# Late weight forms and retention operands given out in parts behind a bank's copy, and halo loads put into the chain of loads

## The chip, the core and the metric

The kernel runs on one core of a Trainium2 chip. The metric is the device time of one execution in microseconds (us); lower is better. Engines are named as in the profile: PE is TensorE (matmuls; PEld its weight loads), ACT is ScalarE, DVE is VectorE, SP the engine that issues most DMAs.

## What is computed

One block over 16 meta tokens and 512 tokens of width 1024: a recurrent branch, a retention branch with four heads, two gates that mix them, an out-projection and a gated feed-forward part with a short convolution. Cut to what matters here:

```python
xn = rms_norm(h, norm_mix_g[l])
z = xn @ w_in[l]
u_rnn, u_gate, q, k, v, g_ret, ga, gb = jnp.split(z, IN_SPLITS, axis=-1)
...
o = retention(q, k, v.reshape(bsz, t, RET_HEADS, RET_DV))
o_b = head_rms(o).reshape(bsz, t, RET_HEADS * RET_DV) * jax.nn.silu(g_ret)
mixed = (jax.nn.sigmoid(ga) * (o_a @ w_branch_rnn[l])
         + jax.nn.sigmoid(gb) * (o_b @ w_branch_ret[l]))
h = h + mixed @ w_out[l]
xn = rms_norm(h, norm_ffn_g[l])
up = causal_dwconv(xn @ w_up[l], ffn_conv_w[l], ffn_conv_b[l])
gate, val = jnp.split(up, 2, axis=-1)
h = h + (jax.nn.gelu(gate) * val) @ w_down[l]
```

## The kernel before

Every f32 operand is held as two f16 halves, hi and lo, and a product is three matmuls (hi by hi, hi by lo, lo by hi). `split` (L90) makes a pair of halves: ACT writes hi (L91), then DVE writes lo (L92). It is used for the weights, for activations and for the values `v`.

**Weights.** They come in units of up to 1 MB. `load` (L96) issues each unit's DMA on SP into a `raw` tile and keeps these loads in one chain of order; a load can go out once its `raw` tile is free. Each unit has a list of steps, and `tick` hands out the next step if not too many tiles (`ahead`) would be held; `get(u)` hands out all that unit u still needs.

**Fast units.** The gates (g_ret, ga, gb), the branch product with w_branch_ret and the down-projection multiply 2x2 blocks with seven products in place of eight. The weights of such a unit need five steps (`fast_steps`, L212): the split of B11, the split of B21 and B22, three sums on DVE in `raw` (L231 to L233), and then two *late forms*: T1 with T3, and T4 with T2, each a split of 128x1024. `fast_products` (L768) is the generator of the seven products P1, P7, P6, P2, P5, P3, P4. P1, P6, P5 and P3 all add into one PSUM bank, `pa`; after P1 and P6 `keep` copies it on ACT to `kept`, after P5 to `last` (L781), and the next of these products may only write the bank when that copy is through. A product of a gate is 12 matmuls of 257 columns; `mix_products` (L970), the product with w_branch_ret, takes two units and has 24 matmuls in each.

**Gates of the retention.** `gated(h)` (L916) runs two gate units of head h and puts the four groups of `retention_out(h+1)` (24 matmuls `ps<-sc,v` each) between their products. At a unit's end `finish` multiplies the gate into the retention's output (L887), and after the second of the two calls `ob_forms` (L893) makes the operands of the later product: four subtractions on DVE (L897 to L900) and four splits into `ob` tiles. `values(h)` (L816) makes `v` in five blocks, each split out of a PSUM bank. Head 3's gates stand among the mixing gates: `gate_a` and `gate_b` call gate products, a branch product and, in `gate_b`, `mix_products`.

**Order.** Each engine runs its own instructions in order. The order is made when the program is built, by a scheduler that takes the program as it is written and the edges of order that the code states; `issue_after` states such an edge without a wait on another engine. The halo columns (two rows of the meta tokens, `hs`, L1066) are needed by `halo_sum` (L1081), in the second out-projection group.

## Time and profile before

| | |
|---|---|
| median of 3 runs | 1076.42 us (1076.34 to 1076.59) |
| profiled execution, its own time | 1076.25 us |
| its span in the trace | 1074.5 us |
| granted TensorE clock | 0.999 |
| PE busy | 1055.9 us, 98% of the span |
| DVE busy | 839.0 us, 78% |
| ACT busy | 567.5 us, 53% |

The profiled execution's time is the span plus 1.75 us that lie around it. Busy shares are for the whole span; the matmuls' ends are modelled.

### The profile page before, as it was taken

To read this page: it belongs to the slowest core of one execution; us is meant where nothing else is said; L and a number is where in the kernel's file an instruction comes from. 1 tells how busy PE (TensorE), PEld (TensorE's weight loads), DVE (VectorE), ACT (ScalarE), POOL (GpSimd) and SP (SyncE) were. 2 spreads that over 40 slices of the span, in tenths; PEclk is the share of its full clock that TensorE was granted. 3 is DMA by queue.
4 is the path that set the end of the run, shared out by engine and by line. 5 is a ranking of instruction groups with operands and counts; after the bars stand their busy time and mean duration, and the time that the engine had idled before them with its cause. 6 is when DMAs were issued, how large, how long until landed. Compare 5 with 4: busy or idle time off the path is not lost.

```text
span 1074.5 us, 20950 instructions
## 1 busy us (share of the span) xinstructions
PE 1055.9 (98%) x9037; PEld 855.1 (80%) x9037; DVE 839.0 (78%) x1219; ACT 567.5 (53%) x847; POOL 6.8 (1%) x20
## 2 busy tenths in 40 slices
PE   8999999999999999999999999999999999999997
PEld 5888888865684858888888885588888888888885
DVE  6875799998786969878697785578767777888875
ACT  6558954435564747566454453365444544454442
POOL 2000000000000000000000000000000000000000
PEclk9999999999999999999999999999999999999999
DMA  7432243431212212423333355143232323113322
GB/s 220 133 117 80 80 138 119 157 120 40 80 41 72 88 62 65 128 89 119 103 104 119 118 200 174 38 159 118 79 118 80 119 79 118 41 60 126 111 79 79
DMA packets 108027, 112.00 MB, mean 104 GB/s; under 512 B 5546, under 2 KB 99472, under 8 KB 107936
## 3 DMA queue, kind: packets, MB, share of 16 engines
q1 hardware_dynamic: 107504, 110.27, 31.4%
q8 instruction: 70, 1.15, 0.4%
q10 hardware_dynamic: 144, 0.26, 0.1%
q0 software_dynamic: 288, 0.14, 0.1%
q14 instruction: 21, 0.17, 0.0%
HBM read 108.57 MB, written 2.10 MB: 103 GB/s over the span
## 4 chain that ended last, share of the span: by engine, by line
PE 75%; DVE 14%; ACT 8%; issue 2%; DMA 1%; SPq 0%; ACTq 0%; DVEq 0%
PE ps L370 33%; PE P L1240 9%; PE pa L776 9%; PE ps L839 4%; PE pm L370 4%; PE ps L1112 4%; PE pe L776 4%; DVE wt L92 3%; PE ps L383 3%; PE pb L776 2%; ACT wt L91 2%; PE ps L861 1%; DVE rnn L575 1%; DVE raw L231 1%; ACT L627 1%
## 5 line engine op out<-in xcount | busy, mean ns | idle before, releaser
L370 PEld LDWEIGHTS <-wt 128*128 128x128 f16 x4224 | 410.5, 97 | 63.7 <-DVE t L667 1.4
L92 DVE SCALAR_TENSOR_TENSOR wt<-raw,wt 128x1024 f16<-128x1024 f32 (+2 forms) x270 | 296.6, 1111 | 71.5 <-ACT wt L91 69.5
L91 ACT ACTIVATE wt<-raw 128x1024 f16<-128x1024 f32 (+2 forms) x270 | 256.4, 965 | 161.1 <-PE ps L370 28.3
L776 PEld LDWEIGHTS <-wt 128*128 128x128 f16 x2016 | 195.0, 97 | 36.0 <-issue 8.8
L370 PE MATMUL ps<-x2h,wt 128*128 128x258 f16 x1440 | 218.8, 273 | 0.0
L370 PE MATMUL ps<-xh,wt 128*128 128x257 f16 (+2 forms) x1056 | 163.8, 275 | 1.1 <-DVE t L667 1.1
L370 PE MATMUL ps<-x2l,wt 128*128 128x258 f16 x720 | 137.7, 272 | 0.0
L1197 DVE SCALAR_TENSOR_TENSOR cv<-ps,vt,cv 128x512 f32<-128x512 f32 x96 | 71.9, 749 | 54.7 <-ACT cv L1195 53.4
L370 PE MATMUL ps<-xl,wt 128*128 128x257 f16 (+2 forms) x528 | 102.2, 275 | 0.0
L1240 PE MATMUL P<-wt,act 128*128 128x256 f16 x792 | 88.3, 273 | 0.0
L1240 PEld LDWEIGHTS <-act 128*128 128x128 f16 x792 | 77.5, 98 | 9.0
L839 PE MATMUL ps<-wt,xh 128*128 128x512 f16 x256 | 76.4, 379 | 1.2 <-DVE v L92 1.0
L776 PE MATMUL pa<-xs,wt 128*128 128x257 f16 x576 | 71.6, 273 | 4.8 <-ACT kept L781 4.5
L1195 ACT ACTIVATE cv<-ps,vt,vt 128x512 f32<-128x512 f32 x48 | 37.1, 773 | 56.8 <-PE ps L370 52.2
L370 PE MATMUL pm<-oa,wt 128*128 128x257 f16 x480 | 55.4, 274 | 0.0
L839 PEld LDWEIGHTS <-xh 128*128 128x128 f16 x256 | 24.8, 98 | 30.9 <-issue 2.9
L839 PE MATMUL ps<-wt,xl 128*128 128x512 f16 x128 | 48.5, 379 | 0.0
L776 PE MATMUL pa<-ob,wt 128*128 128x257 f16 x384 | 45.7, 274 | 0.6 <-ACT last L781 0.5
L1112 PE MATMUL ps<-wt,mx 128*128 128x512 f16 x192 | 44.3, 379 | 0.0
L231 DVE TENSOR_TENSOR raw<-raw 128x1024 f32<-128x1024 f32 x35 | 42.7, 1220 | 0.6
L1112 PEld LDWEIGHTS <-mx 128*128 128x128 f16 x192 | 17.6, 98 | 18.5
L861 PE MATMUL ps<-sc,v 128*128 128x257 f16 (+4 forms) x384 | 32.1, 236 | 0.0
(250 smaller groups left out, 1273.5 us busy)
## 6 DMA issues: line engine op xcount, KB each, us to landing
raw<-in_w_in SPq DMA_DIRECT2D x41, 1024.0 KB, 4.8
raw<-in_w_up SPq DMA_DIRECT2D x24, 1024.0 KB, 5.0
raw<-in_w_down SPq DMA_DIRECT2D x48, 256.0 KB, 3.4
raw<-in_w_branch_ret SPq DMA_DIRECT2D x16, 512.0 KB, 4.3
raw<-in_w_branch_rnn SPq DMA_DIRECT2D x8, 640.0 KB, 4.2
raw<-in_w_out SPq DMA_DIRECT2D x4, 1024.0 KB, 4.9
xin<-in_x SPq DMA_DIRECT2D x4, 512.0 KB, 4.9
h<-in_x SPq DMA_DIRECT2D x4, 512.0 KB, 4.3
```

Source lines behind the costliest of these rows:

```text
L91: nc.scalar.activation(hi, src, AF.Copy, scale=s)
L92: nc.vector.scalar_tensor_tensor(lo, src, s, hi, op0=ALU.mult, op1=ALU.subtract)
L231: nc.vector.tensor_tensor(pair, pair, rv[:, :, right].rearrange("p (h k) c -> p h k c", h=2), op=ALU.add)
L370: nc.tensor.matmul(ps[:, hf, :n], w(aw, k, col, P), src(ax, k, c0, n), start=k == 0 and (aw, ax) == (0, 0), stop=k == nk - 1 and aw == 1)
L383: mm = nc.tensor.matmul(ps[:, hf, :n], w(aw, k, col, P), src(ax, k, c0, n), start=k == 0 and (aw, ax) == (0, 0), stop=k == KD - 1 and aw == 1)
L776: nc.tensor.matmul(ps[:, :257], ws[k // 4](wf, aw, k % 4), src(xf_, ax, k), start=first and k == 0 and (aw, ax) == (0, 0), stop=k == last_ ...
L839: nc.tensor.matmul(pb, xf(ax, k, XF + j0, nb), w(aw, k % 4, 0, 512), start=i == 0, stop=i == 23)
L861: nc.tensor.matmul(ps[:, hf, s0 - lo_i:257], vt[b][:, va, d * P:(d + 1) * P], st[SCP[b][0]][:, sa, o:o + hi_i - s0], start=i == 0, stop=i ...
L1112: nc.tensor.matmul(ps[:, n], mx[k][:, a, c0:c0 + P], wo[k // 2](aw, k % 2, n * 512, 512), start=k == 0 and (a, aw) == (0, 0), stop=k == ks ...
L1195: nc.scalar.activation(vv_, ps[:, :, 2:258], AF.Identity, scale=vt2[:, 96 + ch:97 + ch], bias=b_ff[:, ch:ch + 1])
L1197: nc.vector.scalar_tensor_tensor(vv_, ps[:, :, j:j + 256], vt2[:, 48 * j + ch:48 * j + ch + 1], vv_, op0=ALU.mult, op1=ALU.add)
L1240: nc.tensor.matmul(pd[:, 256 * tt:256 * tt + 256], t[:, ax, c0 + tt * P:c0 + tt * P + P], w(wf, aw, i), start=q % 6 == 0 and tt == 0 and i ...
```

## The change

Four things. The two late forms of a fast unit, and the operands that `ob_forms` makes, carry an edge of order behind the last `keep` copy that was written before them. `tick` after P1 and after P7 hands out no late form. `ob_forms` no longer emits its work at once: it returns three parts (differences, plain, formed), and `flush` emits one part after each of P7, P6 and P5 and after each block of `values`, and what is left before `gate_b`. The two `hs` loads go through `load`, so they stand in the chain of loads at their place in the code. Instruction counts are the same.

```diff
@@ fast_steps
+        def late(run):
+            def behind():
+                with behind_copy():
+                    run()
+            behind.late = True
+            return behind
+
         wviews.append(form)
         return [cut(top, left), cut(low, slice(0, 2 * bc)), sums,
-                cut(top, slice(0, 2 * bc)), cut(low, slice(0, 2 * bc))]
+                late(cut(top, slice(0, 2 * bc))), late(cut(low, slice(0, 2 * bc)))]
 
     steps = []
+    last_keep = [None]
+
+    def behind_copy():
+
+        return nullcontext() if last_keep[0] is None else tc.issue_after(last_keep[0])
+
...
-    def tick(n=1):
+    def tick(n=1, late=True):
...
             if sum(unit_tiles(i) for i in range(current[0], u + 1)) > ahead[0]:
                 return
+            if not late and hasattr(steps[done[0]][1], "late"):
+                return
             emit_step()
...
         def keep(dst, ps):
-            nc.scalar.activation(dst, ps[:, :257], AF.Copy)
+            last_keep[0] = nc.scalar.activation(dst, ps[:, :257], AF.Copy).ins
...
             split(vt[b][:, 0], vt[b][:, 1], pb, S_V / (SW * S_XN))
+            flush()
             tick()
         vv[h] = vt
...
             if j == 0:
-                ob_forms(h, i, ot[2 * i], ot[2 * i + 1])
+                pending.extend(ob_forms(h, i, ot[2 * i], ot[2 * i + 1]))
...
+        def differences():
+            d, y = tmp["d"], tmp["y"] = wtile("d"), wtile("y")
+            nc.vector.tensor_tensor(d[:, :TQ], t0, t1, op=ALU.subtract)
...
+        def plain():
+            if i == 0:
+                ob_a11.append(piece([P, 2, TQ], F16, "ob11"))
+            a11 = ob_a11[h]
+            split(a11[:, 0, 257 * i:257 * i + 257], a11[:, 1, 257 * i:257 * i + 257], t0[:, h0], S_OB)
+            at["A11"] = (a11, 257 * i)
+            halves(t1, S_OB, ("A12", "A22"))
+
+        def formed():
+            halves(tmp["y"], S_OB, ("F7", "F3"))
+            halves(tmp["d"], -S_OB, ("F6", "F5"))
+
+        return [differences, plain, formed]
+
+    pending = []
+
+    def flush(n=1):
+
+        for _ in range(min(n, len(pending))):
+            with behind_copy():
+                pending.pop(0)()
+
+    def advance(run, *names):
+        for nm in names:
+            next(run)
+            if nm in ("P7", "P6", "P5"):
+                flush()
+            tick(1, nm not in ("P1", "P7"))
...
-            for _ in range(2):
-                next(a)
-                tick()
+            advance(a, "P7", "P6")
             next(other)
             scale_head(h, i)
-            for _ in range(2):
-                next(a)
-                tick()
+            advance(a, "P2", "P5")
...
     mix_first(5, branch(u_ba, oa_of, NR))
+    flush(3)
...
         run = mix_unit(u_gb, i)
-        advance(run, 3)
+        advance(run, "P1", "P7", "P6")
         ahead[0] = 12
-        advance(run, 2)
+        advance(run, "P2", "P5")
...
     for t in range(2):
-        nc.sync.dma_start(hs[:, 0, :, t], meta[NM - 2 + t].rearrange("(c p) -> p c", p=P))
+        load(hs[:, 0, :, t], meta[NM - 2 + t].rearrange("(c p) -> p c", p=P))
```

(The four `differences` subtractions and the body of `halves` are those of L897 to L900 and L906 to L909. `gated` and the mixing code call the new `advance` with the products' names.)

On ACT, the second gate unit of head 0, from the silu of the first unit on (`g` is the gate's tile, `wt` a weight tile's hi half, `or` and `sq` the copies of a retention group). Before:

```order
L814 ACTIVATE g_3586<-g_3586 128x514
L91 ACTIVATE ob_3775<-or_3462 128x257
L91 ACTIVATE ob<-or_3463 128x514
L91 ACTIVATE wt<-raw 128x1024
L781 ACTIVATE kept<-pa 128x257
L91 ACTIVATE ob<-y 128x514
L91 ACTIVATE ob<-d 128x514
L865 ACTIVATE or_3644<-ps 128x514
L867 ACTIVATE sq<-ps 128x514
L781 ACTIVATE kept<-pa 128x257
```

The same place on ACT after the change:

```order
L830 ACTIVATE g_3586<-g_3586 128x514
L797 ACTIVATE kept<-pa 128x257
L91 ACTIVATE wt<-raw 128x1024
L797 ACTIVATE kept<-pa 128x257
L91 ACTIVATE ob_3827<-or_3462 128x257
L91 ACTIVATE ob<-or_3463 128x514
L882 ACTIVATE or_3644<-ps 128x514
L884 ACTIVATE sq<-ps 128x514
L91 ACTIVATE wt<-raw 128x1024 x2
L797 ACTIVATE last<-pa 128x257
L91 ACTIVATE ob<-y 128x514
```

The first copy out of the bank went ahead of two `ob` halves and a weight form, and `ob` went behind the second copy. On PE, P6 of this unit now stands directly behind P7; the 24 matmuls of a retention group that stood between them come later.

On ACT, the last gate unit ahead of the first `mix_products` and the start of the latter, from the gate's `last` copy on. Tiles 6230 and earlier belong to the first of its two units of weights; those made from `raw_6161` to the second, and 6275 is that one's T4 and T2. `kept_6278` is the copy after P1 of `mix_products`, `wt_6310` the next gate's. Before:

```order
L781 ACTIVATE last_6144<-pa_6147 128x257
L91 ACTIVATE wt_6275<-raw_6161 128x1024
L814 ACTIVATE g1_6146<-g1_6146 128x257
L814 ACTIVATE g1_6146<-pa_6147 128x257
L91 ACTIVATE wt_6310<-raw_6261 128x512
```

After, in the same stretch:

```order
L797 ACTIVATE last_6144<-pa_6147 128x257
L91 ACTIVATE wt_6230<-raw_6032 128x1024
L830 ACTIVATE g1_6146<-g1_6146 128x257
L91 ACTIVATE wt_6263<-raw_6161 128x512
L830 ACTIVATE g1_6146<-pa_6147 128x257
L91 ACTIVATE wt_6266<-raw_6161 128x1024
L91 ACTIVATE wt_6272<-raw_6161 128x1024
L830 ACTIVATE g0_6145<-g0_6145 128x514
L797 ACTIVATE kept_6278<-pa_6282 128x257
L91 ACTIVATE wt_6275<-raw_6161 128x1024
L91 ACTIVATE wt_6310<-raw_6261 128x512
```

`wt_6275` came directly behind the gate's `last` copy; now it comes behind the first copy of `mix_products`, with four other weight forms between. On PE its P6 is cut: 14 matmuls, 4 of P2, and then the other 10.

On SP, the start of the program. Before:

```order
L102 DMA gmix<-in_norm_mix_g 128x1024
L1068 DMA hs<-in_meta_tokens 128x8x1 x2
L102 DMA xmeta<-in_meta_tokens 128x128
L102 DMA xmeta<-in_norm_mix_g 8x128
L102 DMA raw<-in_w_in 128x8x128
```

and the place on SP where the halo loads stand after the change:

```order
L1102 DMA h_7783<-in_x 128x1024
L102 DMA raw<-in_w_out 128x2x1024 x2
L102 DMA hs<-in_meta_tokens 128x8x1 x2
L102 DMA raw<-in_w_out 128x2x1024
L102 DMA raw<-in_w_up 128x8x256
```

They left the place between `gmix` and `xmeta` and stand ahead of the last quarter of `w_out`. From the out-projection on, PE, ACT and DVE have the order that they had.

## Rows read from the trace of the kernel before

**Rows 1.** The page, its first part (busy time, share and instructions of PE) and its fourth (the chain that ended last, by engine).

```profile
PE 1055.9 (98%) x9037; PEld 855.1 (80%) x9037; DVE 839.0 (78%) x1219; ACT 567.5 (53%) x847; POOL 6.8 (1%) x20
...
PE 75%; DVE 14%; ACT 8%; issue 2%; DMA 1%; SPq 0%; ACTq 0%; DVEq 0%
```

**Rows 2.** Waits of PE: what waited for what, us in total, times, the longest.

```profile
PE pa L776 <- ACT kept L781: 4.5, 8, 1.0
PE ptr L412 <- DVE xn L403: 1.7, 1, 1.7
...
PE ps L839 <- DVE v L92: 1.0, 2, 0.5
...
PE pa L776 <- ACT last L781: 0.5, 1, 0.5
```

**Rows 3.** Busy time by engine in the stretch from 280 to 716 us (gates, retention, mixing, out-projection), the sum of six windows.

```profile
sum 436.00, PE 428.64 PEld 336.17 DVE 332.60 ACT 236.55 POOL 0.00; mean PE 71.44 PEld 56.03 DVE 55.43 ACT 39.43 POOL 0.00
```

**Rows 4.** Timeline of the second gate unit of head 0 (309 to 315 us), ACT's rows first, then DVE's, then PE's: start, duration, engine, line, form; in brackets the idle time before and its releaser.

```profile
309.67 0.63 ACT L814 ACTIVATE g<-g 128x514 f32<-128x514 f32 x1
312.01 0.94 ACT L91 ACTIVATE ob<-or 128x257 f16<-128x257 f32 x2 [1.71 <-DVE or L887]
313.20 1.06 ACT L91 ACTIVATE wt<-raw 128x1024 f16<-128x1024 f32 x1 [0.25 <-DVE raw L231]
314.17 0.37 ACT L781 ACTIVATE kept<-pa 128x257 f32<-128x257 f32 x1
...
311.28 0.69 DVE L887 TENSOR_TENSOR or<-g,or 128x514 f32<-128x514 f32 x1
...
310.90 2.00 PE L861 MATMUL ps<-sc,v 128*128 128x257 f16 x24
...
314.58 1.49 PE L776 MATMUL pa<-xs,wt 128*128 128x257 f16 x12 [0.78 <-ACT kept L781]
```

**Rows 5.** Timeline of ACT, then of PE, a mixing gate's first copy (545 to 548 us).

```profile
545.74 1.06 ACT L91 ACTIVATE wt<-raw 128x1024 f16<-128x1024 f32 x1 [1.90 <-DVE raw L233]
546.71 0.62 ACT L91 ACTIVATE mx<-m 128x514 f16<-128x514 f32 x1
547.23 0.37 ACT L781 ACTIVATE kept<-pa 128x257 f32<-128x257 f32 x1
...
546.77 0.27 PE L776 MATMUL pb<-xh,wt 128*128 128x257 f16 x1
547.64 0.82 PE L776 MATMUL pa<-xs,wt 128*128 128x257 f16 x6 [0.61 <-ACT kept L781]
```

**Rows 6.** Timeline of ACT, then of DVE, in `values(2)` (329 to 333 us).

```profile
329.37 0.63 ACT L91 ACTIVATE ob<-d 128x514 f16<-128x514 f32 x1
329.91 0.58 ACT L91 ACTIVATE v<-ps 128x512 f16<-128x512 f32 x1
...
331.60 0.68 DVE L92 SCALAR_TENSOR_TENSOR v<-ps,v 128x512 f16<-128x512 f32 x1
```

**Rows 7.** Groups by line and form: count, busy us, mean ns of one, idle time before and its releasers.

```profile
L91 ACT ACTIVATE wt<-raw 128x1024 f16<-128x1024 f32 x211 | 219.9, 1052 | 131.1 <-PE P L1240 23.7 <-PE ps L370 22.6 <-DMA raw<-in_w_in 18.1
...
L92 DVE SCALAR_TENSOR_TENSOR wt<-raw,wt 128x1024 f16<-128x1024 f32 x211 | 256.1, 1219 | 53.3 <-ACT wt L91 51.6
...
L231 DVE TENSOR_TENSOR raw<-raw 128x1024 f32<-128x1024 f32 x35 | 42.7, 1220 | 0.6
...
L233 DVE TENSOR_TENSOR raw<-raw 128x512 f32<-128x512 f32 x35 | 24.0, 686 | 0.5
```

**Rows 8.** Timeline of ACT, then of PE, then of DVE, end of a mixing gate and start of `mix_products(0)` (519 to 532 us).

```profile
520.17 0.39 ACT L781 ACTIVATE last<-pa 128x257 f32<-128x257 f32 x1 [2.33 <-PE pa L776]
520.45 1.05 ACT L91 ACTIVATE wt<-raw 128x1024 f16<-128x1024 f32 x1
521.40 0.41 ACT L814 ACTIVATE g<-g 128x257 f32<-128x257 f32 x1
...
528.12 2.80 PE L776 MATMUL pa<-ob,wt 128*128 128x257 f16 x24
...
521.53 1.23 DVE L92 SCALAR_TENSOR_TENSOR wt<-raw,wt 128x1024 f16<-128x1024 f32 x1 [0.52 <-ACT wt L91]
```

**Rows 9.** Timeline of SP's queue, then of DVE, then of PE, at the program's start.

```profile
2.78 1.23 SPq L1068 DMA_DIRECT2D hs<-in_meta_tokens  x2
4.05 3.48 SPq L102 DMA_DIRECT2D xmeta<-in_meta_tokens  x1
...
7.87 1.41 DVE L403 SCALAR_TENSOR_TENSOR xn<-xin,rs,gmix 128x512 f32<-128x512 f32 x2 [1.07 <-DMA gmix<-in_norm_mix_g]
...
8.77 1.23 PE L412 MATMUL ptr<-ident,xn 128*128 128x128 f32 x8 [1.69 <-DVE xn L403]
```

**Rows 10.** The last quarters of `w_out` and the halo: the DMA issues of the page (KB each, us from issue to landing), then timelines of DVE and PE, and what works on the tile `hs` (durations in ns, first and last start).

```profile
raw<-in_w_out SPq DMA_DIRECT2D x4, 1024.0 KB, 4.9
...
hs<-in_meta_tokens SPq DMA_DIRECT2D x2, 4.0 KB, 5.5
...
650.33 1.22 DVE L92 SCALAR_TENSOR_TENSOR wt<-raw,wt 128x1024 f16<-128x1024 f32 x1
...
651.08 11.17 PE L1112 MATMUL ps<-wt,mx 128*128 128x512 f16 x51
...
L1085 DVE SCALAR_TENSOR_TENSOR hs<-ps,hs x2: 164/164/165, 676.2 to 676.9; 128x16 f32<-128x16 f32 x2
```

More of the change, by code (lines that the diff above doesn't have):

```diff
@@ L1 @@
-from contextlib import ExitStack
+from contextlib import ExitStack, nullcontext
 import concourse.bass as bass
@@ L895, in ob_forms, with halves @@
         h0, h1 = slice(0, 257), slice(257, TQ)
-        d, y = wtile("d"), wtile("y")
-        nc.vector.tensor_tensor(d[:, :TQ], t0, t1, op=ALU.subtract)
-        nc.vector.tensor_tensor(y[:, h0], t0[:, h0], t0[:, h1], op=ALU.subtract)
-        nc.vector.tensor_tensor(y[:, h1], d[:, h0], d[:, h1], op=ALU.subtract)
-        nc.vector.tensor_tensor(d[:, h0], t0[:, h0], d[:, h1], op=ALU.subtract)
-        if i == 0:
-            ob_a11.append(piece([P, 2, TQ], F16, "ob11"))
-        a11 = ob_a11[h]
-        split(a11[:, 0, 257 * i:257 * i + 257], a11[:, 1, 257 * i:257 * i + 257], t0[:, h0], S_OB)
-        at = {"A11": (a11, 257 * i)}
-        for src, s, nms in ((t1, S_OB, ("A12", "A22")), (y, S_OB, ("F7", "F3")), (d, -S_OB, ("F6", "F5"))):
+        at = {}
+        tmp = {}
+        ob.append(at)
+        def differences():
+            d, y = tmp["d"], tmp["y"] = wtile("d"), wtile("y")
+            nc.vector.tensor_tensor(d[:, :TQ], t0, t1, op=ALU.subtract)
+            nc.vector.tensor_tensor(y[:, h0], t0[:, h0], t0[:, h1], op=ALU.subtract)
+            nc.vector.tensor_tensor(y[:, h1], d[:, h0], d[:, h1], op=ALU.subtract)
+            nc.vector.tensor_tensor(d[:, h0], t0[:, h0], d[:, h1], op=ALU.subtract)
+        def halves(src, s, nms):
             t = piece([P, 2, TQ], F16, "ob")
@@ L909, in ob_forms @@
             at.update({nm: (t, 257 * n) for n, nm in enumerate(nms)})
-        ob.append(at)
+        def plain():
[20 more added lines that the diff above has]
+            tick(1, nm not in ("P1", "P7"))
     def scale_head(h, i):
@@ L1001, in mix_first @@
         mix_a.append(m)
-    def advance(run, n):
-        for _ in range(n):
-            next(run)
-            tick()
     def rest(run):
@@ L1015, in gate_a @@
             next(run)
-        advance(run, 4)
+        advance(run, "P7", "P6", "P2", "P5")
         ps = branch(u_ba, oa_of, NR)
@@ L1026, in hybrid_block_kernel @@
             head_norm(3)
-        advance(run, 2)
+        advance(run, "P7", "P6")
         ps = branch(u_ba, oa_of, NR)
@@ L1030, in hybrid_block_kernel @@
         scale_head(3, i)
-        advance(run, 2)
+        advance(run, "P2", "P5")
         after = mix_unit(u_ga, i + 1)
@@ L1041, in gate_b @@
         run = mix_unit(u_gb, i)
-        advance(run, 3)
+        advance(run, "P1", "P7", "P6")
         ahead[0] = 12
-        advance(run, 2)
+        advance(run, "P2", "P5")
         rest(run)
```

## The prediction

> **What bounds the kernel now.** The page's first part comes first: PE is busy for 1055.9 of 1074.5 us, and three quarters of the chain that ended last is its own work [rows 1]. The instructions and their counts stay as they are, so all that can be won is PE's idle time, 1074.5 − 1055.9 = 18.6 us, and the next view is what PE waits for [rows 2]: 4.5 us in eight waits for a copy out of the bank (`kept`), 1.7 us once at the start, 1.0 us in two waits for `v`, 0.5 us for `last`. The windows from 280 to 716 us, where the moved work lies, hold 436.00 − 428.64 = 7.36 us of idle [rows 3]. That is the size of the matter: 0.7% of the time.
>
> A matmul of 257 columns follows the last at (2.80 − 0.27) / 23 = 0.11 us in PE's row of 24 [rows 8], but the profile draws each 0.27 long. So a wait is longer than its bracket: PE's last start before a wait is 546.77, the next 547.64, and 0.87 − 0.11 = 0.76 were lost where the bracket has 0.61 [rows 5]. I add 0.16 per wait: 4.5 + 8 × 0.16 = 5.8 us for the copies, 1.0 + 2 × 0.16 = 1.3 us for `v`.
>
> [...] By the brackets alone the two terms would be 5.5 in place of 7.1.
>
> Why the copies are late is seen in the second gate unit of head 0 [rows 4]. The product before the copy had ended when PE went on to `ps<-sc,v` at 310.90 at the latest. ACT was idle for 1.71 us up to 312.01, held at an `ob` half whose input DVE made only at 311.28 + 0.69; then came two `ob` halves (the first row's x2), a late form of 1.06, and the copy at 314.17. PE went on at 314.58. In a mixing gate a late form and an `mx` half stood ahead in the same way [rows 5]. In `values(2)` the hi half of `v` began at 329.91, behind an `ob` half, and its lo half at 331.60, on a DVE that had `ob` work before it [rows 6].
>
> **The change, part by part.**
>
> *Copies ahead of forms (−5.8).* After the change the copy stands directly behind the silu at the place of [rows 4], and ahead of the weight form in the mixing gates. A copy takes 0.37 [rows 4], begins when its product is through, and a whole product (12 × 0.11 = 1.3 us) lies between it and the product that needs the bank. All eight waits should go. What stays: the silu itself stands behind one weight form more, so it ends near 309.67 + 0.63 + 1.05 [rows 4, 7] = 311.4 at the most, and the copy near 311.7, where PE wants the bank at 310.90, since P6 now follows P7 directly and the retention group no longer covers. I take +0.3 over all second units (bounds 0 and three units × 0.7 = 2.1).
>
> *Parts of `ob` by product and by block (−1.3).* In `values` one part goes out per block, behind an earlier copy; a block lasts 24 matmuls of 512 columns, 24 × 2 × 0.11 = 5.3 us, and a part is at most two halves of 0.63 on ACT and two of about 0.7 on DVE [rows 6]. `v` then waits for at most one part, and two banks are in turn. I take both waits as gone; bounds 0 and −1.3. The four subtractions and the splits come later by about one unit, and their reader, `mix_products`, comes after all four heads: P6 there begins at 528.12 [rows 8], P1 and P7 take 2 × 24 × 0.11 before it. Head 3's last part goes out by `flush(3)`, a whole gate of seven products (7 × 1.3 = 9 us) ahead of that. That costs nothing.
>
> *Late forms later: the new wait (+2.4).* The last form of the second w_branch_ret unit (`wt_6275`) came directly behind the gate's `last` copy, so its hi half was made at 520.45 and its lo half ended at 521.53 + 1.23 = 522.76 [rows 8]. P6 of `mix_products` begins at 528.12 and needs this form from its 13th matmul on. Now four forms stand ahead of it, and it is tied to the copy after P1. I lay the new order out with the durations of [rows 7], from the copy at 520.17 on. ACT is soon ahead, DVE sets the pace: lo of `wt_6230` to 522.76, the half-size lo of `wt_6263` 523.4, sums L231 to 524.5, the gate's addition 524.9, lo of `wt_6266` 526.0, of `wt_6272` 527.1, L232 and L233 to 528.3. Only then can hi of `wt_6275` run, 528.4 to 529.5, and lo to 530.7. PE comes to its 15th matmul, the first that reads lo, at 528.12 + 14 × 0.11 = 529.66, and four matmuls of P2 that now stand between take it to 530.1. So 0.6 us are lost, and there are four such places (the four calls of `gate_b`): 2.4 us. Bounds: 0, if DVE runs the subtractions of that stretch in a better order or the forms before have gained on it, and one form of 1.22 each, 4.9.
>
> *`last` copies behind forms (+0.8).* In the third and fourth `mix_products` weight forms of the next units precede the `last` copy. Those of the fourth are of `w_out`, which has to land first. The kernel before has one such wait, 0.5 [rows 2]. I take +0.7 and +0.1; bounds 0 and 2.
>
> *Halo loads (−0.4).* At the start the two loads hold SP for 1.23 us and `xmeta` behind them for 3.48; DVE waits 1.07 for `gmix`, PE 1.69 for `xn` [rows 9]. `gmix` was issued before them, so it can gain only by what their packets share with its own. I take −0.4 (later transposes included); bounds 0 and −1.5 (the 1.07 and 0.4 for later transposes). At the other end they stand ahead of the last quarter of `w_out`, and could hold it by 1.23 + 3.48 = 4.7 us as they held `xmeta`. In the trace of before the last lo half of `w_out` ends at 650.33 + 1.22 = 651.6, and the first out-projection group, which starts at 651.08, reaches k = 7 and 6 after 36 of its 48 matmuls, 36 × 11.17 / 51 = 7.9 us later, at 659. Slack 7.4 us, over the 4.7; nothing. The halo itself is wanted at 676.2 [rows 10], 17 us after the 659 at which the load behind it is wanted, against 5.5 to land.
>
> Sum: −5.8 + 0.3 − 1.3 + 2.4 + 0.8 − 0.4 = −4.0. From the profiled execution's 1076.25 that gives 1072.25. The median of the runs lies 0.17 over the profiled execution; with it, **1072.4 us**.
>
> [...]
>
> **The rivals.**
>
> A, the full gain. The late forms of `mix_products` are ready in time, because ACT and DVE, busy for 237 and 333 of 436 us [rows 3], have room to run ahead. Then 1076.25 − 5.8 − 1.3 − 0.4 + 0.3 + 0.17 = 1069.2. For it: the room. Against it: the edge binds them to the copy whatever room there is.
>
> B, the wait changes place. Each of the four `mix_products` loses a whole form (4.9) and the `last` copies 2: −5.8 + 0.3 − 1.3 + 4.9 + 2 − 0.4 = −0.3, that is 1076.1. For it: the chain above ends on DVE, which has no gap in it. A part of the same case is that the edge does nothing for the time, since a copy that is first in the queue may still wait for its product: then the time stays at 1076.4.
>
> C, slower, by one mechanism: a late form keeps its `raw` tile, the tile's next load starts later, and its landing (4.9 for `w_out` [rows 10]) goes past what PE wants. The `raw` tile of `wt_6275` comes free at 530.7 in place of 522.8, 8 us later. The place where it decides is the last quarter of `w_out`: 8 us and the 4.7 of the halo loads against 7.4 of slack lose 5.3. With B's terms, 1076.1 + 5.3 = 1081.4; with the forecast's, 1077.7. I say 1079. It decides from a landing over 7.4 us later than before. Against it: the loads of `w_out` follow several units after the late ones, and a chain that is 8 us late at one unit gains again where SP had idle time.
>
> [...]
>
> **How the numbers follow.** Forecast 0.45, A 0.18, B 0.25, C 0.12. The range 1068.8 to 1076.8 takes in A, the forecast with its bounds, and B, and leaves out C and a little at the lower end. From run to run a difference of 0.2%, 2.15 us, is about what a measurement of this kernel can tell from no change; faster is below 1074.3. A falls there, and nearly all of the forecast (0.42 of 0.45), and a little of B (0.03): 0.63. Slower is C and 0.02 of B, 0.14. The rest, 0.23, is the same.
>
> **What would show it.** In the profile after: the wait of `pa` for `kept` gone from PE's waits, or under 1 us; the wait for `v` gone; a new wait of `pa<-ob` for DVE's `wt`, about four times 0.4 to 0.6; PE's idle time from 280 to 716 us down from 7.4 to about 4; `xn` at the start earlier by some tenths; the halo's issue near 640 us without a wait for `w_out` in the out-projection. It is wrong if `kept` still waits (the forms were not the cause), if the new wait is much over 0.6 at each place (B), or if PE waits for a form that waits for a load (C).

## The result

| | median | runs |
|---|---|---|
| before | 1076.59 us | 16 (1076.15 to 1078.28) |
| changed | 1079.78 us | 16 (1077.89 to 1085.01) |

The ratio is 1.0031, with a 95% interval of 1.0022 to 1.0040: the change makes the kernel slower by 0.3%. The forecast was 1072.4, the range 1068.8 to 1076.8. The profiled execution of the changed kernel took 1084.24 us (span 1082.5), one of its two slowest; its mean granted clock is 0.994. Over the 16 runs the time goes with that clock: the two at 0.994 took 1084.2 and 1085.0, the five at 0.997 1079.9 to 1081.2, the nine at 0.998 or 0.999 1077.9 to 1079.9.

The busy times and the clock of the page of the changed kernel (its first and second part, in 40 slices of the span):

```profile
PE 1060.5 (98%) x9037; PEld 856.4 (79%) x9037; DVE 839.3 (78%) x1219; ACT 563.5 (52%) x847; POOL 6.9 (1%) x20
...
PEclk8999999999999999999999999999999999999999
```

PE now has 22.0 us of idle time in its span, against 18.6 [rows 1], and 4.6 us more of busy time for the same matmuls. What it waits for:

```profile
PE ptr L428 <- DVE xn L419: 3.2, 1, 3.2
PE ps L855 <- DVE v L92: 2.5, 2, 1.2
PE pa L792 <- ACT last L797: 2.3, 1, 2.3
PE pa L792 <- DVE wt L92: 1.7, 4, 0.4
...
PE pa L792 <- ACT kept L797: 1.3, 3, 0.6
```

Against [rows 2] the wait for `kept` fell from 4.5 to 1.3, as was meant. In its place the first transposes wait 3.2 for `xn` (1.7 before), `values` waits 2.5 for `v` (1.0), the fourth `mix_products` 2.3 for `last` (0.5), and there is a wait for a weight form, four times 0.4, that was not there.

Three matmuls that both kernels have show where the time went. M1 is the one that waits for `t` (L667 before, L683 after), M2 the first of P6 in `mix_products(0)`, M3 the first of the out-projection. The rows of before, then those of after, from PE's timelines:

```profile
162.58 0.40 PE L370 MATMUL ps<-xh,wt 128*128 128x257 f16 x2 [1.11 <-DVE t L667]
```

```profile
166.55 0.40 PE L386 MATMUL ps<-xh,wt 128*128 128x257 f16 x2 [1.12 <-DVE t L683]
...
531.00 1.76 PE L792 MATMUL pa<-ob,wt 128*128 128x257 f16 x14
...
659.23 5.99 PE L1150 MATMUL ps<-wt,mx 128*128 128x512 f16 x27
```

M2 was at 528.12 [rows 8], M3 at 651.08 [rows 10]. So the start lost 3.97; from M1 to M2 the changed kernel gained 365.54 − 364.45 = 1.09; from M2 to M3 it lost 128.23 − 122.96 = 5.27; behind M3 the two differ by 0.15 (1082.5 − 659.23 against 1074.5 − 651.08). The sum of the three is 8.15 us. That is this one execution's loss; the median's is 3.2. The profiled execution is 4.5 over the median, and the two stretches at half clock that are shown below account for about 2.6 and 1.65 of that. In the experiments the same three steps are given as start, middle and end, each against before.

**The start.** SP's queue, DVE and PE of the changed kernel, and PE's windows from 10 to 14 us (busy time of PE, PEld, DVE, ACT, POOL, then the granted clock, the DMA share and GB/s):

```profile
2.30 0.43 SPq L102 DMA_DIRECT2D gmix<-in_norm_mix_g  x1
2.77 0.43 SPq L102 DMA_DIRECT2D xmeta<-in_meta_tokens  x1
3.25 0.38 SPq L102 DMA_DIRECT2D xmeta<-in_norm_mix_g  x1
3.67 0.40 SPq L102 DMA_DIRECT2D raw<-in_w_in  x1
4.10 0.77 SPq L102 DMA_DIRECT2D xin<-in_x  x1
...
9.24 1.41 DVE L419 SCALAR_TENSOR_TENSOR xn<-xin,rs,gmix 128x512 f32<-128x512 f32 x2 [2.33 <-DMA gmix<-in_norm_mix_g]
...
10.14 1.23 PE L428 MATMUL ptr<-ident,xn 128*128 128x128 f32 x8 [3.15 <-DVE xn L419]
```

```profile
10.00:12.00 2.00, 1.86 (x10) 1.34 (x10) 1.96 (x4) 1.19 (x2) 1.00 (x2) 0.81 1.07 374
12.00:14.00 2.00, 2.00 (x9) 1.51 (x9) 1.90 (x6) 0.78 (x2) 0.51 (x1) 0.50 1.09 390
```

`gmix` is issued at the same 2.30, but `xmeta` no longer holds SP from 4.05 on for 3.48 us [rows 9], so the first `w_in` load and the third `xin` go out at 3.67 and 4.10 while `gmix` is still landing. In the kernel before, the first of these two was issued here:

```profile
7.99 0.38 SPq L102 DMA_DIRECT2D raw<-in_w_in  x1
```

`gmix` lands 1.4 us later (9.24 against 7.87, by the start of `xn`), PE is idle for 3.15 us, and then its clock is granted at half, until about 18 us.

**The end of mixing.** SP, ACT and PE of the changed kernel at the fourth `mix_products`, and a window behind it:

```profile
643.82 2.65 SPq L102 DMA_DIRECT2D raw<-in_w_out  x2
646.52 1.90 SPq L102 DMA_DIRECT2D hs<-in_meta_tokens  x2
...
649.94 2.00 ACT L91 ACTIVATE wt<-raw 128x1024 f16<-128x1024 f32 x2 [4.39 <-DMA raw<-in_w_out]
651.85 0.37 ACT L797 ACTIVATE last<-pa 128x257 f32<-128x257 f32 x1
...
652.26 4.47 PE L792 MATMUL pa<-ob,wt 128*128 128x257 f16 x24 [2.28 <-ACT last L797]
```

```profile
653.00:656.00 3.00, 3.00 (x16) 2.10 (x15) 2.28 (x4) 1.45 (x2) 0.00 (x0) 0.50 0.39 116
```

ACT stands for 4.39 us at a form of `w_out` whose load has not landed; the copy `last` is behind it in the queue, and PE behind the copy. Afterwards 24 matmuls took 4.47 us, against 2.80 at full clock [rows 8]. The same load, form and copy in the kernel before:

```profile
634.46 8.70 SPq L102 DMA_DIRECT2D raw<-in_w_out  x3
...
639.31 2.00 ACT L91 ACTIVATE wt<-raw 128x1024 f16<-128x1024 f32 x2 [3.45 <-DMA raw<-in_w_out]
...
645.33 0.39 ACT L781 ACTIVATE last<-pa 128x257 f32<-128x257 f32 x1 [0.27 <-PE pa L776]
```

There ACT waited for the load as well, but its two forms let the next instruction in after 1.91 us (as 649.94 to 651.85 above), at 641.22, and that is 4.11 us ahead of `last`.

**The middle.** In `values(2)` ACT, DVE and PE of the changed kernel:

```profile
331.00 0.42 ACT L91 ACTIVATE ob<-or 128x257 f16<-128x257 f32 x1 [1.63 <-DVE or L904]
331.32 0.58 ACT L91 ACTIVATE v<-ps 128x512 f16<-128x512 f32 x1
...
330.28 0.68 DVE L904 TENSOR_TENSOR or<-g,or 128x514 f32<-128x514 f32 x1
...
332.77 0.68 DVE L92 SCALAR_TENSOR_TENSOR v<-ps,v 128x512 f16<-128x512 f32 x1
...
333.50 0.59 PE L855 MATMUL ps<-wt,xh 128*128 128x512 f16 x2 [1.23 <-DVE v L92]
```

An `ob` half still stands ahead of `v` on ACT and waits for DVE, as in [rows 6]; on DVE a sum of a weight unit (L232) and the subtractions of a part now stand ahead of `v`'s lo half. In `mix_products(0)` ACT, then PE:

```profile
531.25 2.52 ACT L91 ACTIVATE wt<-raw 128x1024 f16<-128x1024 f32 x3 [2.08 <-DVE raw L233]
...
528.08 3.08 PE L792 MATMUL pe<-ob,wt 128*128 128x257 f16 x24
...
533.62 1.27 PE L792 MATMUL pa<-ob,wt 128*128 128x257 f16 x10 [0.43 <-DVE wt L92]
```

The last form's hi half begins at 531.25, behind the sums on DVE, and PE waits at the 15th matmul of P6, as forecast. The product before it (P7) also lost: 3.08 against 2.80 for its 24 matmuls.

### The profile page after: what moved, and what is told of

It is laid out like the page before. It is cut to its first block, busy times and chain, and to the rows that moved or that the text cites. A ratio compares the mean times of both kernels' runs of the same rounds, so it can differ in the third digit from the quotient of the medians.

```text
span 1082.5 us, 20904 instructions
## 1 busy us (share of the span) xinstructions
PE 1060.5 (98%) x9037; PEld 856.4 (79%) x9037; DVE 839.3 (78%) x1219; ACT 563.5 (52%) x847; POOL 6.9 (1%) x20
## 3 DMA queue, kind: packets, MB, share of 16 engines
q8 instruction: 70, 1.15, 0.4%
## 4 chain that ended last, share of the span: by engine, by line
PE 72%; DVE 16%; ACT 7%; DMA 3%; issue 2%; SPq 0%; DVEq 0%; ACTq 0%
PE ps L386 34%; PE P L1278 9%; DVE wt L92 6%; PE pa L792 6%; PE ps L855 5%; PE ps L1150 4%; PE pm L386 3%; PE ps L399 3%; PE pe L792 2%; ACT wt L91 2%; PE pb L792 2%; DMA raw<-in_w_in 1%; PE ps L878 1%; DVE raw L231 1%; DVE rnn L591 1%
## 5 line engine op out<-in xcount | busy, mean ns | idle before, releaser
L91 ACT ACTIVATE wt<-raw 128x1024 f16<-128x1024 f32 (+2 forms) x270 | 253.3, 963 | 136.6 <-DMA raw<-in_w_in 29.4
L792 PE MATMUL pa<-ob,wt 128*128 128x257 f16 x384 | 48.2, 280 | 4.1 <-ACT last L797 2.3
```

The lines of the kernel that those rows point to most:

```text
L91: nc.scalar.activation(hi, src, AF.Copy, scale=s)
L792: nc.tensor.matmul(ps[:, :257], ws[k // 4](wf, aw, k % 4), src(xf_, ax, k), start=first and k == 0 and (aw, ax) == (0, 0), stop=k == last_ ...
```

## The experiments

Theory T had three parts: the halo loads had kept other loads away from `gmix`; the edge on weight forms delays the forms of the w_branch_ret units and, through their `raw` tiles, the loads of `w_out`; the edge behind the last bank copy has no force in `values`. The rivals were chance (S), the halo loads as the cause of the late `w_out` (H), and others that each expectation names. The columns of the table are worked out from M1, M2 and M3 in each kernel's profile.

| kernel | median us | ratio to before, 95% interval | start | middle | end |
|---|---|---|---|---|---|
| changed | 1079.78 | 1.0022 to 1.0040 | +3.97 | −1.09 | +5.27 |
| e1 halo at the start | 1078.82 | 1.0013 to 1.0032 | +0.19 | −0.91 | +2.53 |
| e2 before, halo in the chain | 1076.69 | 1.0000 to 1.0017 | +0.82 | +0.04 | +0.04 |
| e3 changed, gmix second | 1080.11 | 1.0020 to 1.0045 | +0.33 | −1.05 | +4.75 |
| e4 w_branch_ret without edge | 1077.21 | 0.9997 to 1.0014 | +0.33 | +0.35 | +0.48 |
| e5 v tied, edge moved | 1080.87 | 1.0026 to 1.0052 | −0.08 | +1.50 | +2.65 |
| e8 ob parts alone | 1074.31 | 0.9973 to 0.9991 | +0.03 | −1.93 | −0.02 |
| e9 changed, more warming | 1081.76 | 1.0027 to 1.0051 | +1.36 | −0.86 | +3.66 |
| e10 late forms alone | 1079.65 | 1.0018 to 1.0043 | +0.31 | +0.29 | +2.54 |
| e12 edge on gates of heads 0 to 2 | 1080.62 | 1.0026 to 1.0051 | +0.12 | +4.18 | −0.02 |
| e13 ob parts, tied behind v | 1072.57 | 0.9952 to 0.9979 | +0.17 | −3.67 | −0.02 |
| e14 the same, gmix second | 1073.08 | 0.9958 to 0.9981 | +0.64 | −3.54 | −0.03 |

**e1, halo at the start.** The changed kernel with

```diff
-        load(hs[:, 0, :, t], meta[NM - 2 + t].rearrange("(c p) -> p c", p=P))
+        nc.sync.dma_start(hs[:, 0, :, t], meta[NM - 2 + t].rearrange("(c p) -> p c", p=P))
```

> The changed kernel with the two halo loads back at the program's start, ahead of xmeta. Theory T: at the start the halo loads were a brake that kept the first w_in loads and the third and fourth xin loads from competing with gmix; with them back xn begins near 7.9 us again, PE waits for it 1.7 and not 3.2, the granted clock stays at 1.0, and the 3.96 us that the start lost in the profile are back. The late w_out loads are not the halo's doing, so the wait of pa for last of about 2.3 us at the fourth mix_products stays. Median 1077 to 1078, against 1079.8. Rival S (the late xn was chance): as the changed kernel, 1079.8. Rival H (the halo loads hold the last quarters of w_out): the wait for last falls under 0.6 as well, and the median to 1074 or less.

The start is that of before, within 0.2, and 1 us of the median came back, less than the profile's 3.8. At the end 2.53 of 5.27 stay. ACT of this kernel:

```profile
645.25 2.00 ACT L91 ACTIVATE wt<-raw 128x1024 f16<-128x1024 f32 x2 [3.17 <-DMA raw<-in_w_out]
```

ACT still waits for `w_out`, but 1.2 us less (3.17 against 4.39), and PE's wait for `last` is at most 1.1. So T and H each own a part of it; e2, next, shows that the halo loads alone cost nothing there. The median missed its expectation by 0.8.

**e2, the halo loads alone.** The kernel before with the edit of e1 turned round.

> The kernel before with nothing changed but the two halo loads put into the chain of loads. Theory T: xn begins 1.3 to 1.5 us later than before, at 9.1 to 9.4; PE's wait of over 3 us brings the granted clock to half for some us; 1.4 us slower without the lower clock, 4 us with it: median 1078 to 1080.6. No wait for w_out at the end of mixing. Rival S: same as before, 1076.6. Rival H: a wait for last or for a w_out form near 650 us, and as much slower.

```profile
8.99 1.41 DVE L403 SCALAR_TENSOR_TENSOR xn<-xin,rs,gmix 128x512 f32<-128x512 f32 x2 [2.29 <-DMA gmix<-in_norm_mix_g]
```

`xn` was late again, by 1.1, without any other edit, which speaks against S; the profiled run lost 0.8 with it. But the median is only 0.2 over before, and below the 1078 expected. The runs range from 1076.4 to 1080.4: four of twelve lie over 1078. One reason stands in the two profiles. In the changed kernel the warming matmuls (18 that keep PE busy until `xn` is there) run 0.43 us apart at first and 0.22 apart from 4.45 us on, and the 18 of them took 5.48 us. In e2 they took 6.52, which by the same two spacings puts the change at about 6.5, an estimate; and with `xn` nearly as late (8.99 against 9.24) PE's gap was 1.87 in place of 3.15, with no half clock behind it. That the unprofiled runs of e2 differ by this is likely and not shown. At the end e2 lost nothing (+0.04), so rival H is not the whole of it: the late `w_out` needs the rest of the change.

**e9, more warming.** The changed kernel with

```diff
-    keep_warm(18)
+    keep_warm(30)
```

> The changed kernel with 30 in place of 18 warming matmuls ahead of the first transposes (12 x 0.21 = 2.6 us more on PE, up to about 9.6 us, while it waits for xn anyway). The part of theory T on the clock: the half clock from 10 to 18 us comes from PE's idle time of over 3 us, so it stays at 1.0 now, and of the 3.96 us at the start some 2.5 come back; in the profile the transposes take 0.1 us each and not 0.2. Median about 1 to 2.5 us under the changed kernel's. Rival (the clock drops for another cause, such as the traffic at the start): the half clock stays, the time too.

PE's timeline and its windows at the start:

```profile
5.75 5.03 PE L443 MATMUL ps<-warm 128*128 128x512 f16 x20
10.61 1.04 PE L428 MATMUL ptr<-ident,xn 128*128 128x128 f32 x8
```

```profile
10.00:12.00 2.00, 2.00 (x15) 1.40 (x13) 1.97 (x4) 0.75 (x2) 0.66 (x2) 1.00 1.07 374
12.00:14.00 2.00, 2.00 (x16) 1.56 (x16) 1.90 (x6) 1.38 (x4) 0.51 (x1) 1.00 1.08 390
```

The transposes came 0.5 later than in the changed kernel, yet with no idle time ahead of them the clock stayed at 1.00, and the start lost 1.36 in place of 3.97. With the same late `gmix` and the same traffic (374 and 390 GB/s in both kernels) the half clock is thus the idle time's doing, and about 2.6 of the 3.97. The median did not come as expected: 1081.76 of five runs, 2 us over the changed kernel and not 1 to 2.5 under it. In the profile the end lost 3.66; why its other runs are slower was not profiled.

**e4, the edge off the w_branch_ret units.** e1, and in `fast_steps`

```diff
+        def wrap(run):
+            return run if len(loaded) - 1 in u_bb else late(run)
...
-                late(cut(top, slice(0, 2 * bc))), late(cut(low, slice(0, 2 * bc)))]
+                wrap(cut(top, slice(0, 2 * bc))), wrap(cut(low, slice(0, 2 * bc)))]
```

> The changed kernel with the halo loads back at the start, and with the late forms of the w_branch_ret units handed out as before (no edge behind a copy for these eight units; the gates keep it). Theory T: the edge on these units delays their second unit's forms (four waits for DVE's wt, 0.42 each, and 0.6 more lost by the same delay in each mix_products) and, since their raw tiles come free late, the loads of w_out (issue 635.7 and 643.8 us, against 625.5 and 634.5 before), which is the wait of 2.3 for last. All of that goes: median 1072 to 1074, faster than before by 0.25 to 0.4%. Rival H: the w_out wait was the halo loads' and the gain over the halo-at-start kernel is only the four waits, 1.7. Rival G (the gates' own late forms make the raw tiles late): the wait for last stays above 1 us.

The waits for a weight form in `mix_products` and the longer wait for `last` are gone, as T has it, and the end is nearly that of before. But new waits for `kept` stand at the gates of the mixing part, 1.56 us at 516.64, 0.27 at 548.00 and 1.14 at 565.46; with the four between 412 and 477 us that e1 has too, the waits for `kept` are 4.4 us in all. Ahead of the first of the three, ACT reads:

```profile
513.79 2.52 ACT L91 ACTIVATE wt<-raw 128x1024 f16<-128x1024 f32 x3 [0.45 <-PE pa L795]
516.22 0.36 ACT L800 ACTIVATE kept<-pa 128x257 f32<-128x257 f32 x1
```

Three weight forms in a row stand ahead of the copy there. The gain expected (1072 to 1074) did not come, and the median is 1077.21. My reading, argued and not tested: ACT and DVE have this work to do by then; the gates' own forms wait for copies, so work without an edge gathers in front of the next copy, and with an edge it is too late for P6.

**e5, v tied, and e12.** e5 is e1 with the parts in `values` behind v's own halves; the edit also set the edge that weight forms use:

```diff
-            split(vt[b][:, 0], vt[b][:, 1], pb, S_V / (SW * S_XN))
-            flush()
+            hi, lo = split(vt[b][:, 0], vt[b][:, 1], pb, S_V / (SW * S_XN))
+            last_keep[0] = hi.ins
+            with tc.issue_after(lo.ins):
+                flush()
```

> The kernel with the halo loads at the start, and in values the operand parts are tied behind the block's own v (behind its hi half on ACT and its lo half on DVE) in place of the last bank copy. Theory T: the edge behind the last copy means nothing in values, where no copy is made, so the scheduler put ob work ahead of v there again, and each of the two waits for v grew to 1.4 to 1.5 us of PE; with the tie both go, 2.9 us: median about 1076 against 1078.8. Rival V (v is late for its own reasons, such as weight forms on DVE): the waits stay above 1 us in sum, median within 1 us of 1078.8.

The wait for `v` in `values` fell from 2.6 to 0.5 in two, which is T, though two waits for `v` at the sums of the scores (L895) came in, 0.8 together. The median rose by 2 over e1, where a fall to 1076 was expected, for another reason, new waits that end at 287 and 298 us:

```profile
PE ps L895 <- DVE ssum L888: 1.3, 1, 1.3
PE ps L880 <- DVE sf L735: 0.9, 1, 0.9
```

`last_keep` now named a half of `v` in `values(0)` and `values(1)` as well, so weight forms were held behind it and then ran among the scores. The edit was two changes in one.

e12 is e5 with the edge kept for the units `u_gr` of heads 0 to 2 only.

> The kernel of the tied v, with the edge and the rule on late forms kept only for the six gate units of heads 0 to 2; the mixing part has the order of before. Theory T: what the retention's gates gain stays (before they lose 0.94, 0.22, 1.16, 0.50, 0.33 and 1.06, 4.2 in sum; of that 1.4 remains), v gains its 1.3, and the mixing loses nothing: 1076.5 - 2.8 - 1.3 = 1072.4, faster than before by 0.3 to 0.4%. Rival V: 1074 or more, with v waits left.

The end is that of before to 0.02, so the end's loss needs the edge on the mixing part's forms. The middle has e5's fault, and more: 4.18, and the median is 8 over the 1072.4 expected. As a test of the retention's gates it is inconclusive.

**e8 and e10, the two halves apart.** Both are e1. e8 leaves the weight forms alone,

```diff
-                late(cut(top, slice(0, 2 * bc))), late(cut(low, slice(0, 2 * bc)))]
+                cut(top, slice(0, 2 * bc)), cut(low, slice(0, 2 * bc))]
```

> The halo loads at the start, the operands of the retention in parts as in the change, but no edge and no rule on weight forms. Theory T: the waits in mix_products (four times 0.27 and 0.59) and the longer wait for last are gone, since those come from the edge on weight forms; the waits for v stay at 1.4 each; the copies of the retention's gates are late by at most a weight form. 1076.5 + 1.6 for v, less 2 to 3 for the copies: 1075 to 1076. Rival O (the parts of ob make the loads late): a wait for last over 1 us stays.

and e10 makes the operands at once:

```diff
-                pending.extend(ob_forms(h, i, ot[2 * i], ot[2 * i + 1]))
+                [run() for run in ob_forms(h, i, ot[2 * i], ot[2 * i + 1])]
```

> The halo loads at the start, the edge and the rule on late weight forms as in the change, but the operands of the retention made all at once as before. Theory T: the four mix_products lose 0.27 and 0.59 each, 3.4, and the wait for last 0.6 more; the waits for v are those of before, 0.65 each; of the copies only those that waited behind weight forms are earlier, 1.5 to 3 us. Median 1078 to 1080, slower than before. Rival O: no loss in mix_products, median under 1076.

e8 came 0.7 under its 1075 to 1076, and e10 within its 1078 to 1080. PE's waits in e8:

```profile
PE ps L855 <- DVE v L92: 2.5, 2, 1.5
...
PE pa L792 <- ACT kept L797: 1.8, 4, 0.6
...
PE pa L792 <- ACT last L797: 0.5, 1, 0.5
```

The parts alone take the wait for `kept` from 4.5 to 1.8 and make the kernel 0.18% faster; the edge on weight forms alone makes it 0.3% slower, nearly all of it at the end (+2.54 of 3.14). By profile the two give −1.92 and +3.14, together +1.2; e1, with both, lost 1.81.

One part of e10's expectation failed. The waits for `v` were to be those of before, 0.65 each; they were 2.03 and 1.56. So the wait for `v` grows by either half alone, to 2.5 with the parts and to 3.6 with the late forms, and is 2.6 with both. That part of theory T, the parts' edge as the one cause, is too narrow. Each half alone also brings the wait for `kept` down, to 1.8 (e8) and 1.6 (e10).

**e13, the parts tied behind v.** e8, and the tie of e5 without the assignment:

```diff
-            flush()
+            with tc.issue_after(hi.ins), tc.issue_after(lo.ins):
+                flush()
```

> The operands of the retention in parts, no edge on weight forms, halo loads at the start; and in values each part is tied behind that block's own v, on ACT and on DVE, without touching the edge behind the bank copy (the kernel with the tied v had moved that edge as well, and so held weight forms behind v from 286 us on). Theory T: the two waits for v (1.67 and 1.15 us lost) fall to 0.4 or less each, the rest is that of the kernel with the parts alone: 1074.3 - 2.2 = 1072.1, 0.4% faster than before. Rival V: v waits are caused by weight forms on DVE: 1074.

```profile
PE pa L792 <- ACT kept L797: 1.3, 3, 0.6
...
PE ps L855 <- DVE v L92: 1.1, 2, 0.6
...
PE pa L792 <- ACT last L797: 0.5, 1, 0.5
```

This version beats both kernels: 1072.57, 0.34% faster than before (0.21 to 0.48%). The time is that expected (1072.1). The wait for `v` is back to 1.1, no better than before, and over the 0.4 each that was expected. On DVE `v`'s lo half now stands behind two sums of a weight unit (L232 at 326.83 and L233, each 0.69), so the rest of that wait looks like rival V's; that was not tested.

**e14 and e3, gmix second.** e13 and the changed kernel, each with

```diff
-    load(xin[0][:, 1], x2[P:2 * P])
     load(gmix, norm_mix_g.partition_broadcast(P))
+    load(xin[0][:, 1], x2[P:2 * P])
```

> The same kernel with the load of gmix issued before the second xin load. Theory T on the start (gmix lands last and shares the DMA engines with what is issued about it): xn begins at 6.9 to 7.3 in place of 7.9, and the first product some tenths to 1 us earlier: 1071.2 to 1072. Rival (the second xin, 1 us later, is what the rest of the start waits for): no change against the kernel without it, within 0.3 us.

> The changed kernel, halo loads in the chain, with gmix issued before the second xin load. Theory T: what made xn late was gmix landing among the w_in and xin loads that the halo loads had held back; with gmix ahead of them xn begins at 7.5 or earlier though nothing holds the others back, PE waits under 2 us for it, the granted clock stays at 1.0, and the profile starts its first product at 14 to 15 and not 19 us. Median 1078 to 1079, that of the kernel with the halo at the start or a little over (the wait for w_out stays, longer by the halo's time on SP). Rival (the halo loads' own absence or the clock is at fault in another way): xn at 9 us again, 1080.

In e14 `xn` began at 7.12, 1.0 before that of e13, and nothing was gained (0.5 us slower, intervals that overlap): PE then waits 0.85 for `xmeta`, and the second `xn` began at 9.95, against 9.64 in e13. So another load bounds the rest of the start, as its rival said. In e3, with the halo loads in the chain and nothing holding the others back, DVE, and ACT at the end:

```profile
7.29 1.42 DVE L419 SCALAR_TENSOR_TENSOR xn<-xin,rs,gmix 128x512 f32<-128x512 f32 x2
```

```profile
647.46 2.00 ACT L91 ACTIVATE wt<-raw 128x1024 f16<-128x1024 f32 x2 [4.46 <-DMA raw<-in_w_out]
```

The start is whole (+0.33). So the late `gmix` was a matter of which loads were in flight with it, not of the halo loads as such. The end lost 4.75 without a half clock, and with it the median, 1080.11, missed its 1078 to 1079: the expectation had the wait for `w_out` a little longer than that of e1, and it was 3.4 against 1.1.

With the edge on the weight forms and the halo at the start the end lost 2.53 (e1), 2.65 (e5) and 2.54 (e10). With the halo in the chain it lost 3.66 (e9), 4.75 (e3), and 5.27 in the changed kernel, of which the half clock is 4.47 − 2.82 = 1.65 and 3.62 the rest. In these single profiles the halo loads in the chain thus go with 1.0 to 2.2 more at the end. The load that decides is the second of `w_out`'s, whose form stands ahead of `last`. From its issue to the form's start:

| | issue | form | between |
|---|---|---|---|
| e1 | 640.35 | 645.25 | 4.9 |
| e10 | 641.70 | 646.57 | 4.9 |
| e5 | 642.50 | 647.50 | 5.0 |
| changed | 643.82 | 649.94 | 6.1 |
| e9 | 641.82 | 647.60 | 5.8 |
| e3 | 640.25 | 647.46 | 7.2 |
| before | 634.46 | 639.31 | 4.9 |
| e2 | 635.37 | 640.26 | 4.9 |

In the changed kernel, e9 and e3 the halo loads are issued while it is in flight (646.52, 644.74 and 644.62), and it is 0.8 to 2.3 us longer under way. In e2 they are so too, at 638.40, and it is not: so the halo loads alone don't make it longer, and what does in the other three stays open.

With this the waits for `last` add up, reckoned from P5, the product whose sum `last` copies (it starts at 642.47 before, 643.69 in e1 and 647.16 in the changed kernel). In the changed kernel the load is issued 643.82 − 634.46 = 9.36 later than before and P5 starts 4.69 later, so the load has fallen back by 4.67 behind PE; in e1 it is 5.89 − 1.22 = 4.67 as well. Against the 4.11 of slack that makes 0.6 with e1's load, and 1.8 with the changed kernel's, which is 1.3 longer under way. PE's wait grew by 1.06 − 0.47 = 0.6 and by 2.28 − 0.47 = 1.8. The 4.67 goes with the late forms: in e4, without the edge on the w_branch_ret units, it is 1.16 − 1.15 = 0.

## Why the prediction was wrong, step by step

The terms as forecast, and as they came in the profile (0.16 added for each wait):

| term | forecast | profile |
|---|---|---|
| copies, with what stays | −5.5 | −4.0 |
| waits for `v` | −1.3 | +1.5 |
| late forms in `mix_products` | +2.4 | +3.5 |
| `last` copies, half clock included | +0.8 | +3.5 |
| halo loads at the start | −0.4 | +4.0 |
| sum | −4.0 | +8.5 |

The span grew by 8.0. Without the 2.6 and 1.65 of half clock the right column would still be +4.2, so the forecast did not fail by the clock alone. Three steps failed: what the halo loads held back at the start, the order in `values`, and the wait of the `last` copy for a late load.

**Copies ahead of forms (−5.8, +0.3 left).** The mechanism is shown (the wait fell from 4.5 to 1.3), the residual was mis-sized. With 0.16 added for each wait, 1.3 + 3 × 0.16 = 1.8 is left, not 0.3. At the place of [rows 4] PE lost nothing. The bound for the silu, one weight form more, was too small at another gate of the retention, where ACT and PE of the changed kernel read:

```profile
413.11 2.53 ACT L91 ACTIVATE wt<-raw 128x1024 f16<-128x1024 f32 x3
415.52 0.64 ACT L830 ACTIVATE g<-g 128x514 f32<-128x514 f32 x1
416.04 0.39 ACT L797 ACTIVATE kept<-pa 128x257 f32<-128x257 f32 x1
...
416.48 1.49 PE L792 MATMUL pa<-xs,wt 128*128 128x257 f16 x12 [0.44 <-ACT kept L797]
```

Three forms stand ahead of the silu, and the copy follows that. At the longest of the three waits (0.63, at 479.83) no form stands there: the silu itself waits 1.57 for DVE's `g`.

**Parts in `values` (−1.3).** Wrong in sign: 2.5 against 1.0 in brackets, 1.5 us lost in place of 1.3 won. The step "a part goes out per block, behind an earlier copy" took the order of the code for the order on the engine. The edge is behind the last bank copy, which is long past in `values`, so the scheduler was free to put `ob` ahead of `v`, and did; tying the parts behind `v` took most of it back (e5, e13). The late forms have a share that the prediction left out: by themselves they make the wait for `v` 3.6 (e10).

**Late forms in `mix_products` (+2.4).** The mechanism is shown by e8 and e4, which take the edge away and with it the waits. The lay-out with DVE as the pace held: hi of the last form was expected (528.4 − 520.17) = 8.2 us behind the `last` copy and came 531.25 − 522.78 = 8.5 behind it. Too small by P7, which I took as free: it needs T3 of the second unit and lost 3.08 − 2.80 = 0.28 at each place, 1.1 in four.

**`last` copies behind forms (+0.8).** The right place, and the wrong size and reason for it. I bounded it at 2 without asking when the `w_out` load would land: it fell back by 4.67 us behind PE, with 4.11 of slack. The wait was 2.3 in the profile, 1.1 in e1 and 3.4 in e3, and in the changed kernel the half clock came on top.

**Halo loads (−0.4, and nothing at the end).** Wrong twice. At the start I asked what the removed loads cost and not what they held back: "it can gain only" had no row behind it, while SP's queue in the trace of before showed which loads stood behind them (the first `w_in` and the third `xin`, issued from 7.99 us on, when `gmix` had landed). At the end I compared a late `w_out` with the out-projection's first use of its last quarter, 659, and found 7.4 us of slack. But the same engine's queue holds the `last` copy behind a `w_out` form, and that copy ran at 645.33 in the kernel before, 13.7 us ahead of 659. The 4.7 itself did not come: in e2 the last quarter is issued at 643.74, against 634.46 + 8.70 − 0.37 = 642.79 before, with PE 0.9 later too.

**Rival C** had the mechanism of the end (late forms, late `raw` tiles, late loads, and the halo's time added), a time of 1079, and a chance of 0.12. It decided at another place than it named: not in the out-projection, but at the fourth `mix_products`. The traces show the copy held by the form ahead of it: `last` took 0.37 us and came 1.9 behind the start of that form (651.85 against 649.94). In e3 the product whose sum it copies had ended at 644.80 + 1.60 = 646.40, and ACT stood idle for the load until 647.46; still the form ran first, and the copy at 649.37.

What stays open: why runs of one kernel differ by up to 7 us. The clock of the runs and the two half-clock stretches of the profile point to PE's long waits. Of the kernels with a long wait at the start or at `last` (changed, e1, e2, e3, e5, e9, e10) 21 of 58 runs have a mean clock of 0.997 or less; of those without (e4, e8, e12, e13, e14) none of 38. But only single runs are profiled.

## What to carry to other kernels

An edge that puts an urgent instruction first also makes everything tied to it late; before adding one, follow what the late work frees (here a buffer, and with it a load) up to the next instruction of the same queue that somebody waits for. A load that looks like dead weight at a program's start may be what keeps other loads away from the one that is needed first (here `xn` began at 7.87 with the halo loads at the start, and at 8.99 and 9.24 without them): look at what is queued behind it before moving it. State an edge behind the thing that must not wait, in the place where it must not, and read the resulting order on both engines.

## What the runs showed of the hardware

PE's idle time can cost twice. In the changed kernel, after 3.15 us without a matmul, the clock was granted at 0.50 from 11.25 to 18.07 us, and after a gap of 2.28 us that ended at 652.26 again from 652.95 to 656.37; with warming matmuls in the first gap it stayed at 1.00 (e9). A wait of 3.4 at the same place in e3 was not followed by a half clock (1.00 in all windows from 644 to 656 us), so a gap's length alone does not decide it.

The changed kernel's clock changes at instants that lie whole steps of 3.41 us apart: the half clock lasted 6.83 and 3.41, and between the two lie 634.88 = 186 × 3.4133. The last change, to 0.50 when PE has no more to do, lies so too, at 1079.62: 423.25 = 124 × 3.4133 behind 656.37. In the kernel before the only change of this kind is at 1072.97, and 1072.97 − 313 × 3.4133 = 4.60 is where its warming matmuls come to run 0.22 us apart (starts at 4.47, 4.76 and 4.97). In the changed kernel they do so between 4.04 and 4.45, and 11.25 − 2 × 3.413 = 4.42.

That the idle time within such a step decides is my estimate from these instants. PE's idle time is counted in steps below; for e2 and e3 the steps are reckoned from the instant at which the warming matmuls come to run 0.22 us apart, itself an estimate from the time that they took (6.5 us in e2, 6.4 in e3).

| kernel | step | PE idle in it | clock in the next |
|---|---|---|---|
| changed | 7.83 to 11.25 | 2.31 | 0.50 |
| changed | 649.54 to 652.95 | 2.28 | 0.50 |
| e2, estimate | 6.52 to 9.93 | 1.87 | 1.00 |
| e3, estimate | 644.68 to 648.09 | 1.68 | 1.00 |
| e3, estimate | 648.09 to 651.51 | 1.70 | 1.00 |

By this reckoning the wait in e3 is cut in two by the end of a step, and neither half is enough: in the table a step with 2.28 us or more idle brought the half clock and one with 1.87 or less did not, with none between. A wait of 2.0 in e10 (for `v`) brought none either: that execution's mean clock is 0.999, that of the kernel before. If the estimate holds, it is in part luck whether a wait of 2 to 3.4 us costs the half clock, as the steps start at another time in each profile (4.42 in the changed kernel, 4.60 before, about 6.5 in e2); no run tests that. Why the half clock lasted two steps at the start and one at the end the traces don't tell.

The second `w_out` load took 4.9 to 5.0 us from its issue to its form where the halo loads were at the start, and 5.8 to 7.2 where they were issued into its flight, 2.7 to 4.4 us behind it (changed, e9, e3). But in e2 they were issued 3.0 us behind it and it took 4.9, so the halo loads alone are not the cause, and the cause stays open.
